# A hybrid S5 and sparse-attention decoder step: filler steps, row copies, key loads and attention side steps put in other places

## The chip, the cores and the metric

One NeuronCore of a Trainium2 chip runs the whole program. The metric is device time of one execution, in microseconds (us); lower is better. The engines are TensorE (PE for matmuls, PEld for its weight loads), VectorE (DVE), ScalarE (ACT), GpSimd (POOL) and SyncE (SP), which here issues nearly all DMAs.

## The reference

One step of a two-layer decoder on 256 new prompt tokens and 8 sample tokens (one for each of 8 sequences with 256 tokens of past), model width 1024, everything in fp32:

- Layer 0: RMS norm, an S5 mixer (64 groups of 16 channels, 64 complex states each, a scan over the 256 tokens), gelu, a gated linear unit (glu, 1024 to 2048), then a squared-ReLU MLP (1024 to 4096 to 1024).
- From its result come shared keys and values in three branches (compressed, selected, window), and queries and gates for layer 1.
- Layer 1: attention of 16 query heads on 4 key/value heads, three softmax branches weighted by sigmoid gates, an output projection and a second MLP.
- Outputs: the tokens, the new cache rows, the shifted window caches of the 8 sequences, and the S5 states.

The attention part, cut to its core:

```python
p_c = masked_softmax(q @ kc)          # 8 compressed blocks of 32 tokens
p_s = masked_softmax(q @ ks)          # selected blocks: with 256 tokens, all of them
p_w = masked_softmax(q @ kw)          # window of 512: all causal tokens
o = g[0] * (p_c @ vc) + g[1] * (p_s @ vs) + g[2] * (p_w @ vw)
win_kv_sample = concat([cache_win_kv, new_row])[:, -256:]    # 255 old rows are copied
```

## The kernel before, in words

**Dense work.** Every dense layer works on all 264 tokens at once, in tiles of 128 output features. `wload` (L594) issues a 512 KB weight load on SP into one of 4 `raw` buffers; `wsplit` (L601) splits it into a high part (ACT, L610) and a rest (DVE, L611); `mm3` (L616) makes three matmuls for each of 8 input blocks (L617 to L619). So a weight tile is 24 matmuls of 264 columns. MLP 0 and MLP 1 have 32 up tiles and 8 down tiles of 4 weight tiles each.

**The S5 stage** (`s5_stage`, L158) is written in a fixed order (`manual_schedule`). Beside it `sample_compress` runs as a generator, `filler(n)` being n steps of it. Its first three steps are loads; then come two streams (keys, values) of nine steps: eight with four matmuls each of cached page rows on the compression weights (L813), in four pairs, and one with biases and gelu. A pair of the first stream, when done, also issues the next weight load, and the second pair the sixteen page rows of a block (L789). `F` says how many steps stand where: `n` behind the first half's chunk matmuls (`chunk_in(0)`), `o` behind the second half's, `q` and `r` later. Behind `n` come `transpose_in(1)` and `chunk_in(1)`; behind `o` the output tables `powers_out` on DVE (L384 to L387), `kernels`, the scan tables, the scan (`up`, `carry`, `down`) and `from_states` (L483), which gives the stage's outputs. The first output table takes the buffer that `transpose_in(1)` reads from.

**Outside that stage** the compiler's planner orders each engine's instructions: it simulates the program with costs of its own and issues what is ready, earlier traced first, so a load whose buffer is free can move far ahead. `issue_after(i)` (here `after(engine)`, the engine's last traced instruction) keeps instructions behind another of the same engine.

**MLP 0** calls `side(m)` after each up tile: one step of `sample_keys` (two of `comp_tail`, then for each of 8 sequences 512 KB of cached keys, L862 and L864) for the first ten tiles, and for every odd m from 17 a copy of one sequence's old window rows from DRAM to DRAM (510 KB), behind SP's last load. It calls `on2(m)` after each down tile; for m = 1 that asks for the four compression weights of 512 KB (`compress_weights`, L1042).

**Before the attention stage** come the key/value tiles, the queries of group 0, the `gates` (L1106: one dense tile of 48 features, a sigmoid at L1118) and `Q1` of the four query tiles of group 1 (`q_dense`, L1135), with steps of the prompt's compression between them (`prompt_compress`, which has a gelu at L1074).

**The attention stage** (`prompt_attn`, L1164) goes through 12 units: for each of 2 groups and 2 head pairs a unit 0 (the first 128 tokens of both heads; scores at L1209 and L1213) and units for the second 128 tokens of each head (L1217, L1220). In round i it makes the scores of unit i, the softmax of unit i-1 (maximum at L1234 on DVE, exponentials at L1236 on ACT, scaling at L1245 on DVE), and transposes (L1254) and values (L1268, L1275) of unit i-2, then calls `side`. There are two score banks of PSUM, which a unit's exponentials set free. `cmp_branch` (L1178 to L1201) is the compressed branch of a group; group 1's must come before unit 6's values. `side` now drives two generators with the counts `SIDE` and `SIDB`: the first goes through the remaining query tiles, the two `q_post` (normalisation, rotary, transposes: two steps each) and `cmp_branch(1)`; the second through `sample_qk` (the sample's query and key norm; DVE lines L1304 to L1339) and the 12 steps of `sample_attn`: value loads and scores (L1381), softmax, transposes, values (L1424, L1428), for each of two halves of the sequences.

**After it** `out_proj` (L1450) makes 8 tiles; the first `SPLIT` = 3 have their group 0 half made early, between the last units. All need the sample's columns of `oh` and `ol`, which are split last in `sample_attn`.

Of the kernel before, what the change touches and what calls it, by code (L numbers as in the profile page):

```python
# [81 lines left out]
F32 = mybir.dt.float32  # L82
F32R = mybir.dt.float32r
I32 = mybir.dt.int32
AF = mybir.ActivationFunctionType
# [66 lines left out]
        pass  # L152


F = dict(n=4, o=5, q=4, r=5)


def s5_stage(K, filler):  # L158
# [356 lines left out]
    chunk_in(0)  # L515
    filler(F["n"])
    powers_in(1)
# [12 lines left out]
    bbar_block(1)  # L530
    filler(F["q"])
    kernels(1)
# [504 lines left out]
def compress_weights(K):  # L1037

    w1v = K.A["cmp_w1"]
    K.w1p = [e8(K, [128, 2, 4, 256], f"w1p{i}") for i in range(2)]  # L1040
    for lc in range(4):
        K.nc.sync.dma_start(K.w1p[lc // 2][:, lc % 2], w1v[0][:, 4 * lc:4 * lc + 4])  # L1042
# [63 lines left out]
def gates(K, xh, xl):  # L1106

    nc = K.nc
    S, V, G = nc.scalar, nc.vector, nc.gpsimd
    at, ak = K.at, K.ak  # L1110
    raw = K.wr.tile([128, 8, 48], F32, tag="raw", name="wg")
    nc.sync.dma_start(raw, K.A["w_gate"])
    pt = K.ps("mm")
    for k, h, l in wsplit(K, raw, parts=[(slice(0, 48), raw)]):
        mm3(nc, pt[0:48, 0:NT], h[:, 0:48], l[:, 0:48], xh[:, k], xl[:, k], k == 0, k == 7)
    g = ak.tile([48, NT], F32, name="gT")
    V.tensor_tensor(g, pt[0:48, 0:NT], K.rstd[0:48], ALU.mult)
    S.activation(g, g, AF.Sigmoid)  # L1118
    K.gp = at.tile([128, 2, 16, 3], F32, name="gp")
    pg = K.ps("tr")  # L1120
    for qt in range(2):
        nc.tensor.transpose(pg[:, 48 * qt:48 * qt + 48], g[:, 8 + 128 * qt:136 + 128 * qt], K.ident[0:48, 0:48])
    S.activation(K.gp.rearrange("p q h b -> p (q h b)"), pg[:, 0:96], AF.Copy)
    K.gs = at.tile([128, 2, 3], F32, name="gs")
    pg = K.ps("tr")
    for bh in range(2):
        lt = ak.tile([48, 4, 32], F32, tag="pct", name="glt", bufs=1)
        V.tensor_tensor(lt, g[:, 4 * bh:4 * bh + 4].unsqueeze(2).to_broadcast([48, 4, 32]),
                        K.cst("maskH")[0:48].unsqueeze(1).to_broadcast([48, 4, 32]), ALU.mult)
        nc.tensor.matmul(pg[:, 4 * bh:4 * bh + 3], lt.rearrange("p b h -> p (b h)"), K.cst("sel3")[0:48],  # L1130
                         start=True, stop=True)
    S.activation(K.gs, pg[:, 0:8].rearrange("p (b x) -> p b x", b=2)[:, :, 0:3], AF.Copy)
# [336 lines left out]
        part(m, (1,) if m < split else (0, 1))  # L1469


def build(ctx, tc, A, O):
    nc = tc.nc
    K = Ctx()
    K.nc, K.tc, K.A, K.O = nc, tc, A, O
    _, off = shape_constants()
# [32 lines left out]
    with ExitStack() as es:  # L1509
# [5 lines left out]
        steps = sample_compress(K)  # L1515
# [24 lines left out]
    with ExitStack() as es:  # L1540
        K.hid = es.enter_context(tc.tile_pool(name="hid", bufs=1))
        kh, kl = pair("kh", "kl", F32R)
        n2 = Norm(K)

        def on2(m):
            split_x(K, x[:, m], kh[:, m], kl[:, m], K.vec[:, 32 + m:33 + m])
            n2.add(x[:, m])
            if m == 1:
                compress_weights(K)
        K.ld = es.enter_context(tc.tile_pool(name="ld", bufs=2))  # L1550
        keys = sample_keys(K)

        def side(m):
            next(keys, None)
            if m == 10:
                with after(nc.gpsimd), after(nc.vector):
                    attn_tables(K)
            if m >= 16 and m % 2:
                b = (m - 16) // 2
                with tc.issue_after([i for i in nc.cur_bb.bb.instructions if i.engine == nc.sync.engine][-1]):  # L1560
                    nc.sync.dma_start(O["win_old"][b], A["cache_win_kv"][b, 1:256])
        mlp(K, 0, xh, xl, n1, x, on2, side)
    phase.close()
    psum(ctx, "pa", PSB)
# [1 line left out]
    with ExitStack() as es:  # L1566
# [3 lines left out]
        with ExitStack() as ek:  # L1570
# [46 lines left out]
            queue1 = []  # L1617
            q1 = q_dense(K, K.qh, K.ql, 1, queue1)
# [7 lines left out]
        oh, ol = ft(F32R, "oh"), ft(F32R, "ol")  # L1626
        with ExitStack() as ek:
            K.aa = ek.enter_context(tc.tile_pool(name="aa", bufs=1))

            def side_a(cmp_branch):  # L1630
                yield from q1
                for q in queue1:
                    yield from q
                cmp_branch(1)
                yield

            def side_b():
                sample_qk(K)
                yield
                yield from sample_attn(K, oh, ol)  # L1640
            steps = []

            def side(i, cmp_branch):
                if not steps:
                    steps.extend([side_a(cmp_branch), side_b()])
                for _ in range(SIDE[i]):
                    next(steps[0], None)
                for _ in range(SIDB[i]):
                    next(steps[1], None)
            prompt_attn(K, oh, ol, side)  # L1650
            for s in steps:
                for _ in s:
                    pass
        yh, yl = ft(F32R, "yh"), ft(F32R, "yl")
        n3 = Norm(K)
# [13 lines left out]
PSC = dict(fl=2, tr=3)  # L1669
PSA = dict(mm=3)  # L1670
PSB = dict(sc=2,po=1)
SIDE = (3,1,1,1,0,0,1,1,1,1,0,0,0,0)
SIDB = (1,2,2,2,2,2,2,2,0,0,0,0,0,0)
Q1 = 2
KVQ = 0
PLAN = ('cccc', 'qqq', 'qqq', 'qq', '', 'c', 'c', 'c', 'c', 'c', '', 'c', 'c', 'c', 'c', 'c')
SPLIT = 3
# [92 lines left out]
```

## Time and profile before

| what | us |
| --- | --- |
| runs | 745.57 median of 3, 744.51 to 746.26 |
| profiled execution | 747.1, its span 745.3 |
| PE busy (6160 matmul records) | 708.7 of the span, 95% |
| DVE, ACT, POOL busy | 526.0, 404.5, 55.7 |
| mean granted clock of PE | 0.956 |
| chain that ended last, by engine | PE 81%, DVE 10%, DMA 4% |

Times in the rows count from the span's start. The granted clock is the share of PE's full 2.4 GHz, so 0.50 is 1.2 GHz. Matmuls are pipelined, and a matmul's duration is longer than its distance to the next: the count of matmuls in a stretch says more of the pace than busy time. Roughly, the S5 stage ends at 106 us, glu at 153, MLP 0 at 350, keys, values and queries at 423, the attention stage at 538 and the rest with the end.

### The profile page before, as it was taken

What the parts mean: (1) busy time and instruction counts of PE and PEld (TensorE: products, weight loads), DVE (VectorE), ACT (ScalarE), POOL (GpSimd) and SP (SyncE); (2) the same over time, 40 slices, a digit from 0 to 9 for tenths busy, and PEclk for the clock granted to TensorE, in tenths of its full rate; (3) what the DMA queues carried; (4) which work ended last, traced back from release to release, by engine and by line L of the source; (5) the groups of instructions that cost most, each with busy time, mean ns of one, the idle gap of its engine ahead of it and who ended that gap; (6) DMA issues with size and microseconds to landing.
All of it is one profiled execution on the core that took longest, in us unless ns stands there. A gap on an engine that the chain in (4) does not pass through costs nothing.

```text
span 745.3 us, 16132 instructions
## 1 busy us (share of the span) xinstructions
PE 708.7 (95%) x6160; PEld 645.8 (87%) x6160; DVE 526.0 (71%) x1154; ACT 404.5 (54%) x918; POOL 55.7 (7%) x103
## 2 busy tenths in 40 slices
PE   3799879999999999999989989999999999999997
PEld 1788769999999999999978955455799999999997
DVE  8969988887677665656777698755488777755553
ACT  5339166656566554545664767444366666644442
POOL 0000001101200000001023141100030000000000
PEclk9699999999999999999999969577999999999999
DMA  7763117657997555555546551000165555565661
GB/s 252 224 183 129 58 60 227 193 166 229 382 320 266 185 185 184 178 191 171 178 158 211 162 183 58 0 1 1 57 195 173 176 191 171 185 192 191 198 188 40
DMA packets 53327, 124.68 MB, mean 167 GB/s; under 512 B 6522, under 2 KB 26874, under 8 KB 52994
## 3 DMA queue, kind: packets, MB, share of 16 engines
q1 hardware_dynamic: 52530, 122.08, 50.1%
q10 hardware_dynamic: 720, 1.58, 0.6%
q8 instruction: 48, 0.79, 0.5%
q14 instruction: 29, 0.24, 0.1%
HBM read 120.63 MB, written 7.18 MB: 171 GB/s over the span
## 4 chain that ended last, share of the span: by engine, by line
PE 81%; DVE 10%; DMA 4%; SPq 2%; issue 1%; ACT 1%; DVEq 0%; ACTq 0%
PE ps_mm L618 22%; PE ps_mm L617 22%; PE ps_mm L619 22%; PE ps_sc L1217 3%; PE ps_tr L1254 2%; PE ps_po L1275 2%; DMA w<-cmp_w_in 1%; DMA raw<-w_up_in 1%; DVE big L466 1%; DVE St L467 1%; PE ps_fl L813 1%; PE ps_mm L1428 1%; SPq L789 1%; PE ps_sc L1220 1%; DVE St L447 1%
## 5 line engine op out<-in xcount | busy, mean ns | idle before, releaser
L611 DVE TENSOR_TENSOR wl<-raw,wh 128x512 fp32r<-128x512 f32 x344 | 241.3, 706 | 147.5 <-ACT wh L610 141.5
L610 ACT ACTIVATE wh<-raw 128x512 fp32r<-128x512 f32 x344 | 215.1, 630 | 200.2 <-PE ps_mm L618 149.4
L617 PE MATMUL ps_mm<-hh,wh 128*128 128x264 f32 x512 | 145.3, 284 | 0.0
L618 PE MATMUL ps_mm<-hl,wh 128*128 128x264 f32 x512 | 145.0, 283 | 0.0
L619 PE MATMUL ps_mm<-hh,wl 128*128 128x264 f32 x512 | 145.0, 283 | 0.0
L618 PEld LDWEIGHTS ps_mm<-hl,wh 128*128 128x128 f32 x512 | 96.5, 188 | 0.0
L617 PEld LDWEIGHTS ps_mm<-hh,wh 128*128 128x128 f32 x512 | 96.4, 188 | 0.0
L619 PEld LDWEIGHTS ps_mm<-hh,wl 128*128 128x128 f32 x512 | 96.0, 187 | 0.0
L617 PE MATMUL ps_mm<-xhxl,wh 128*128 128x264 f32 x256 | 72.7, 285 | 1.2 <-ACT wh L610 1.2
L618 PE MATMUL ps_mm<-xhxl,wh 128*128 128x264 f32 x256 | 73.0, 285 | 0.0
L618 PE MATMUL ps_mm<-yl,wh 128*128 128x264 f32 x256 | 72.9, 285 | 0.0
L619 PE MATMUL ps_mm<-xhxl,wl 128*128 128x264 f32 x256 | 72.4, 284 | 0.4 <-DVE wl L611 0.4
L617 PE MATMUL ps_mm<-yh,wh 128*128 128x264 f32 x256 | 72.6, 284 | 0.0
L619 PE MATMUL ps_mm<-yh,wl 128*128 128x264 f32 x256 | 72.6, 284 | 0.0
L617 PEld LDWEIGHTS ps_mm<-xhxl,wh 128*128 128x128 f32 x256 | 48.2, 188 | 1.7 <-ACT wh L610 1.7
L619 PEld LDWEIGHTS ps_mm<-xhxl,wl 128*128 128x128 f32 x256 | 48.0, 188 | 0.9 <-DVE wl L611 0.9
L617 PEld LDWEIGHTS ps_mm<-yh,wh 128*128 128x128 f32 x256 | 48.2, 188 | 0.0
L619 PEld LDWEIGHTS ps_mm<-yh,wl 128*128 128x128 f32 x256 | 48.2, 188 | 0.0
L618 PEld LDWEIGHTS ps_mm<-xhxl,wh 128*128 128x128 f32 x256 | 48.1, 188 | 0.0
L618 PEld LDWEIGHTS ps_mm<-yl,wh 128*128 128x128 f32 x256 | 48.1, 188 | 0.0
L648 POOL TENSOR_TENSOR nacc<-nacc,sq 128x264 f32<-128x264 f32 x21 | 17.7, 844 | 322.1 <-ACT sq L647 241.4
L1236 ACT ACTIVATE P<-ps_sc,nm 128x128 f32<-128x128 f32 (+1 forms) x64 | 26.3, 427 | 26.9 <-DVE nm L1234 20.2
(438 smaller groups left out, 1471.2 us busy)
## 6 DMA issues: line engine op xcount, KB each, us to landing
raw<-w_up_in SPq DMA_DIRECT2D x64, 512.0 KB, 3.9
raw<-w_down_in SPq DMA_DIRECT2D x64, 512.0 KB, 3.6
raw<-s_w_glu_in SPq DMA_DIRECT2D x16, 512.0 KB, 3.7
w<-cmp_w_in SPq DMA_DIRECT2D x12, 512.0 KB, 4.5
raw<-w_kv_in SPq DMA_DIRECT2D x12, 512.0 KB, 3.7
blk<-cache_cmp_in SPq DMA_DIRECT2D x64, 64.0 KB, 2.1
raw<-w_q_in SPq DMA_DIRECT2D x8, 512.0 KB, 4.0
win_old_out<-cache_win_kv_in SPq DMA_DIRECT2D x8, 510.0 KB, 5.8
```

Source lines behind the costliest of these rows:

```text
L447: TT(o, o, b_, ALU.add)
L466: TT(w, c, m, ALU.mult)
L610: nc.scalar.activation(h[:, :, cols], src[:, c:c + 4], AF.Copy)
L611: nc.vector.tensor_tensor(l[:, :, cols], src[:, c:c + 4], h[:, :, cols].bitcast(F32), ALU.subtract)
L617: nc.tensor.matmul(out, wh, xh, start=start, stop=False)
L618: nc.tensor.matmul(out, wh, xl, start=False, stop=False)
L619: nc.tensor.matmul(out, wl, xh, start=False, stop=stop)
L648: nc.gpsimd.tensor_tensor(self.acc, self.acc, sq, ALU.add)
L1217: nc.tensor.matmul(banks[g2], K.QT[hs[g2], 4 * gp + 2 * rp + u - 1, 128:256], K.KTp[hs[g2], gp], start=True, stop=False)
L1236: S.activation(P[:, i], sv[:, i], AF.Exp, bias=nm[:, i:i + 1], accum_out=den[:, i:i + 1])
L1254: nc.tensor.transpose(pt[:, 128 * j:128 * j + 128], Pf[:, 128 * j:128 * j + 128], K.ident)
L1275: nc.tensor.matmul(po[64 * g2:64 * g2 + 64, 128 * kt:256], K.Vp[:, kt, br, 64 * g:64 * g + 64], rhs, start=False, stop=(br == 1 and kt == 1))
```

## The change

- `F`: two filler steps go from `n` to `o`.
- `gates`: an exponential of one element of the sigmoid's result follows the sigmoid on ACT; nothing reads it.
- The copies of old window rows go from MLP 0's up tiles 17, 19, ... 31 to its down tiles: tile m asks for the copy of sequence m, behind SP's last traced instruction.
- `sample_keys` makes a step after up tiles 0, 1, 2, 3 and then after every even tile, so the ten steps end at m = 14.
- `Q1` is 3: one more query tile of group 1 stands ahead of the attention stage.
- `SIDE` is now a table of letters for each round: a digit is a step of that `q_post`, `q` the last query tile (its PE instructions kept behind PE's last traced ones, the scores of unit 1), `s` is `sample_qk`, `a` a step of `sample_attn`, `d` is `cmp_branch(1)`. Compared with before, `sample_qk` goes from round 0 to 2, `sample_attn` from rounds 1 to 7 to rounds 4 to 10, and `cmp_branch(1)` from round 6 to 4.

```diff
-F = dict(n=4, o=5, q=4, r=5)
+F = dict(n=2, o=7, q=4, r=5)
...
     S.activation(g, g, AF.Sigmoid)
+    S.activation(ak.tile([1, 1], F32, name="tle"), g[0:1, 0:1], AF.Exp)
...
+def one(f, *a):
+
+    f(*a)
+    yield
...
             if m == 1:
                 compress_weights(K)
+            with after(nc.sync):
+                nc.sync.dma_start(O["win_old"][m], A["cache_win_kv"][m, 1:256])
...
         def side(m):
-            next(keys, None)
+            if m < 4 or m % 2 == 0:
+                next(keys, None)
...
-            if m >= 16 and m % 2:
-                b = (m - 16) // 2
-                with tc.issue_after([i for i in nc.cur_bb.bb.instructions if i.engine == nc.sync.engine][-1]):
-                    nc.sync.dma_start(O["win_old"][b], A["cache_win_kv"][b, 1:256])
...
-            def side_a(cmp_branch):
-                yield from q1
-                for q in queue1:
-                    yield from q
-                cmp_branch(1)
-                yield
-
-            def side_b():
-                sample_qk(K)
-                yield
-                yield from sample_attn(K, oh, ol)
-            steps = []
+            steps = {"s": one(sample_qk, K), "a": sample_attn(K, oh, ol)}
...
-                if not steps:
-                    steps.extend([side_a(cmp_branch), side_b()])
-                for _ in range(SIDE[i]):
-                    next(steps[0], None)
-                for _ in range(SIDB[i]):
-                    next(steps[1], None)
+                steps.setdefault("d", one(cmp_branch, 1))
+                for c in SIDE.get(i, ""):
+                    if c == "q":
+                        with after(nc.tensor):
+                            next(q1, None)
+                    else:
+                        next(steps[c] if c in steps else queue1[int(c)], None)
...
-SIDE = (3,1,1,1,0,0,1,1,1,1,0,0,0,0)
-SIDB = (1,2,2,2,2,2,2,2,0,0,0,0,0,0)
-Q1 = 2
+SIDE = {0: "0", 1: "q0", 2: "1s", 3: "1", 4: "ad", 5: "aa", 6: "aa", 7: "aa", 8: "aa", 9: "aa", 10: "a"}
+Q1 = 3
```

## Rows read from the trace of the kernel before

**Rows 1.** The page's second part: granted clock in 40 equal slices, tenths.

```profile
PEclk9699999999999999999999969577999999999999
```

**Rows 2.** Windows of the attention stage: length, then each engine's busy us, clock, DMA.

```profile
434.20:447.80 13.60, 13.60 (x31) 6.41 (x29) 13.13 (x50) 7.02 (x29) 7.58 (x14) 0.50 0.40 137
447.80:468.30 20.50, 19.31 (x123) 11.42 (x122) 17.20 (x53) 13.78 (x58) 3.57 (x13) 1.00 0.16 53
468.30:492.20 23.90, 23.32 (x80) 12.30 (x82) 13.05 (x39) 7.09 (x30) 1.36 (x1) 0.50 0.00 1
505.90:516.10 10.20, 10.20 (x47) 5.00 (x48) 4.99 (x17) 2.04 (x8) 0.00 (x0) 0.50 0.00 0
```

**Rows 3.** The chain of waits, S5 stage: start, length, what.

```profile
35.70 7.55 PE ps_fl L813 x32
43.25 0.45 PE ps_tr L350 x4
```

**Rows 4.** Timeline of PE, end of S5: start, length, what; idle before.

```profile
94.28 0.54 PE L483 MATMUL ps_mm<-St,Fb 128*32 128x72 f32 x21 [2.32 <-DVE St L467]
...
104.47 0.33 PE L483 MATMUL ps_fl<-St,Fb 128*32 128x72 f32 x8 [1.01 <-DVE St L467]
```

**Rows 5.** Timeline of ACT and DVE, S5's second half.

```profile
36.83 0.70 ACT L330 ACTIVATE E<-e 128x512 f32<-128x512 f32 x1
...
45.13 2.29 DVE L384 TENSOR_TENSOR Fc<-Cl,pr 128x2048 f32<-128x2048 f32 x1 [6.26 <-ACT ET L352]
```

**Rows 6.** Windows of MLP 0's up tiles.

```profile
195.00:210.00 15.00, 13.34 (x104) 12.49 (x103) 8.78 (x18) 8.38 (x20) 0.00 (x0) 1.00 0.99 385
230.00:245.00 15.00, 15.00 (x126) 15.00 (x125) 10.70 (x21) 9.61 (x22) 0.00 (x0) 1.00 0.79 269
```

**Rows 7.** Timeline of SP's DMA issues and of ACT, MLP 0.

```profile
191.07 3.95 SPq L1042 DMA_DIRECT2D w1p<-cmp_w_in  x4
195.11 0.99 SPq L597 DMA_DIRECT2D raw<-w_up_in  x2
197.01 0.63 SPq L1561 DMA_DIRECT2D win_old_out<-cache_win_kv_in  x1
...
204.72 0.63 ACT L610 ACTIVATE wh<-raw 128x512 fp32r<-128x512 f32 x1 [2.19 <-DMA raw<-w_up_in]
```

**Rows 8.** Timeline of ACT: table loads around the gates and the first softmax.

```profile
412.06 1.28 ACT L1118 ACT_TABLE_LOAD   x1
...
414.51 1.28 ACT L1074 ACT_TABLE_LOAD   x1
...
430.98 1.28 ACT L1236 ACT_TABLE_LOAD   x1
432.28 0.37 ACT L1236 ACTIVATE P<-ps_sc,nm 128x128 f32<-128x128 f32 x1
```

**Rows 9.** Timeline of PE in the attention stage: units 1 and 7, and transposes.

```profile
433.84 0.89 PE L1217 MATMUL ps_sc<-KTp,QT 64*128 64x512 f32 x1 [1.60 <-ACT P L1236]
...
445.14 1.91 PE L1254 MATMUL ps_tr<-ident,P 128*128 128x128 f32 x8
...
468.88 1.22 PE L1217 MATMUL ps_sc<-KTp,QT 64*128 64x512 f32 x1 [1.71 <-ACT P L1236]
```

**Rows 10.** Groups of DVE instructions by line, 430 to 450 us.

```profile
L1304 DVE TENSOR_SCALAR rs<-sv 128x96 int32<-128x96 int32 x1 | 1.2, 1211 | 0.0
...
L1333 DVE TENSOR_SCALAR ssq<-ssq,gvec 128x16 f32<-128x16 f32 (+1 forms) x3 | 0.6, 231 | 0.0
```

**Rows 11.** Timeline of PE and DVE: the sample's last steps and the output projection.

```profile
509.62 2.07 PE L1424 MATMUL ps_mm<-vnew,ptx 8*128 8x256 f32 x4
511.62 3.64 PE L1428 MATMUL ps_mm<-vr,pts 128*32 128x256 f32 x32
...
520.28 0.22 DVE L627 TENSOR_TENSOR ol<-os,oh 128x64 fp32r<-128x64 f32 x1
...
538.77 0.39 PE L617 MATMUL ps_mm<-oh,wh 128*128 128x264 f32 x1 [0.28 <-DVE x L1463]
```

**Rows 12.** Groups of PE instructions by line, 516 to 538 us.

```profile
L617 PE MATMUL ps_mm<-oh,wh 128*128 128x264 f32 x20 | 5.3, 297 | 0.0
```

More of the change, by code (lines that the diff above doesn't have):

```diff
@@ L1628, in build @@
             K.aa = ek.enter_context(tc.tile_pool(name="aa", bufs=1))
-            def side_a(cmp_branch):
-                yield from q1
-                for q in queue1:
-                    yield from q
-                cmp_branch(1)
-                yield
-            def side_b():
-                sample_qk(K)
-                yield
-                yield from sample_attn(K, oh, ol)
-            steps = []
-            def side(i, cmp_branch):
-                if not steps:
-                    steps.extend([side_a(cmp_branch), side_b()])
-                for _ in range(SIDE[i]):
-                    next(steps[0], None)
-                for _ in range(SIDB[i]):
-                    next(steps[1], None)
+            steps = {"s": one(sample_qk, K), "a": sample_attn(K, oh, ol)}
+            def side(i, cmp_branch):
+                steps.setdefault("d", one(cmp_branch, 1))
[5 more added lines that the diff above has]
+                        next(steps[c] if c in steps else queue1[int(c)], None)
             prompt_attn(K, oh, ol, side)
-            for s in steps:
-                for _ in s:
+            for _ in q1:
+                pass
+            for g in queue1 + [steps[c] for c in "dsa"]:
+                for _ in g:
                     pass
```

## The prediction, made before the result was known

> **What bounds the kernel now.** I read the page first. TensorE is busy for 708.7 of 745.3 us (the table of the profile above), so a saving must take away time in which PE waits or in which it runs slowly; the line of granted clock shows where the second lies: in the second slice, and in the 24th and the 26th to 28th, the attention stage [rows 1]. The windows cut at the changes of clock come next. Three stretches of 13.6, 23.9 and 10.2 us run at 0.50, the 1.2 GHz level, with PE busy almost throughout; those between them run at 2.4 GHz [rows 2]. So 47.7 us are worth 23.9 us if the clock stayed up and nothing else took over. DVE is the engine that would: 13.13 us of the first stretch's 13.6, but only 13.05 of the second's 23.9 and 4.99 of the third's 10.2 [rows 2]. Third, the first 106 us, where the order is written by hand: there DVE's long chain (output powers, scan tables, scan) ends last, and PE's last steps wait for it [rows 3 to 5]. Fourth, MLP 0, the only dense stage in which PE misses matmuls [rows 6].
>
> **The S5 tables.** Four filler steps (32 matmul records) run in 7.55 us on PE between the first half's chunk matmuls and the second half's transposes, 1.89 us a step [rows 3]. The change leaves two there and puts two, 3.78 us, behind the second half's chunk matmuls. The transposes, now at 43.1, could start at 39.5: their input, ACT's copy of E, ends at 36.83 + 0.70 = 37.5 [rows 5]. DVE's first output table had waited 6.26 us for them, until 45.13 [rows 5]; it starts near 41.4 and the DVE chain behind it moves up by 3.8. What is late next is PE: its own steps keep their sum, so its convolutions end where they did and only its waits for the scan can go. They are 2.32 us before the first state outputs and 1.01 us before the last [rows 4]. I take 3.3 us; the ends are 2.3 (the first wait alone) and 3.8 (all of DVE's move). The loads that the moved steps issue on SP (two weight tiles and sixteen page rows) go out up to 4 us later; they are for the second stream of page rows, which PE reaches four filler steps (7.6 us) and the first kernels later. That covers them, and without the cover the price is that same 4 us.
>
> **Row copies and key steps.** PE makes 104 matmuls in 195 to 210 us, where a quiet 15 us has 126 [rows 6]: 22 x 0.119 = 2.6 us lost. SP's order says why: four compression weights (2 MB) at 191.07, then two weight tiles at 195.11, which ACT gets at 204.72 after a wait of 2.19 us; the first row copy, at 197.01, stands behind those tiles [rows 7]. So taking the copies away from here doesn't free the tiles that stall. The new copies stand behind the last load of each down tile, one in 11.4 us (four weight tiles of 24 matmuls at 0.119); in 230 to 245 us they come twice as often and PE loses nothing [rows 6], so I cost them at nothing; were a weight tile held up behind one, the 2.6 us of now are the nearest price. One doesn't move as it seems: that of m = 1 is tied to SP's instruction before it, the last compression weight, which the planner already issues by 195 [rows 7], so it stays in the crowd. The key loads now come by every second tile; the planner issues them when a buffer is free, so their order on SP may hardly change. I take 0.6 us, nearest to the row order; ends +2.6 (the stall goes) and -2.6 (it doubles).
>
> **The attention stage.** No work is added but one exponential of one element. The third tile of the second query group goes ahead of the stage; the fourth (24 matmuls, 2.9 us) is held on PE behind unit 1's scores. Behind it on PE wait unit 2's scores; those first need unit 1's banks, so the tile lies in a wait that is there anyhow, and its query rows are first read by unit 9. If PE isn't waiting there, it costs nothing net either, as the same 2.9 us leave the time before unit 0. Now PE idles 1.60 us before unit 1's scores, waiting for ACT's exponentials, and the clock is at half in the stretch that follows [rows 2, 9]. A dense tile there should bring it back soon. DVE then binds: 13.13 us less the steps of the sample's query norm that move on by two units (1.2 + 0.6 us [rows 10]) is 11.3, so 13.6 can't go under 11.3: 2.3 us. In the second stretch the clock fell after a wait of 1.71 us for ACT before unit 7's scores [rows 9]; nothing is put there, and the sample's steps that come one by one are the same matmuls, later. I count that stretch and the third at nothing. Ends: all three at 2.4 GHz down to DVE's floor, 2.3 + 10.8 + 5.2 = 18.3 us gained; or the 20.5 us stretch falls to half, which costs the 19.3 us that PE is busy in it [rows 2]. I take 2.3, nearest to the stretch that the tile is put into.
>
> **The exponentials' table.** It is loaded at 430.98, 1.28 us, and the first exponential begins at 432.28, while PE stands idle [rows 8]. A tiny exponential behind the gates' sigmoid would move that load, but here the compression's gelu comes after the sigmoid (loads at 412.06 and 414.51 [rows 8]) and would throw the table out again. Then the load at 430.98 stays and one of 1.28 us is added where ACT isn't last. I take 0; ends +1.3 and -1.3. The Trainium skill (ScalarE: Activation LUTs, "Table sets: the hidden batching unit") says the same against this edit: each such function anchors a set of its own and calls are to be grouped by set. Its section "What ACT_TABLE_LOAD costs" puts a switch at 2.66 us, drain included; the row shows 1.30 from the load's start to the next function's, so by the page the ends would be twice as far.
>
> **Sum.** 3.3 + 0.6 + 2.3 + 0 = 6.2 us. The profiled execution took 747.1 (span 745.3 and 1.8 around it), so it would be 740.9; it is 1.5 over the median of the runs, 745.57, from which the same step gives 739.4.
>
> **The rivals.** (a) *The clock stays up further on.* If the calmer order also takes away the wait before unit 7, half of the 16.0 us in the second and third stretches comes on top: 739.4 - 8.0 = 731.4. For it: DVE has room there. Against it: nothing is put at that wait. (b) *Only S5 comes through.* The clock falls as now, or again between units 2 and 4, where the sample's score matmuls no longer stand: 745.57 - 3.9 = 741.7. For it: in the second stretch PE is busy for 23.3 of 23.9 us with scores and transposes and the clock stays down [rows 2]. The Trainium skill (TensorE: Matmul & The Clock Gate, "Part 4: PE-mode transpose") says that transposes don't count as PE-busy in the same way; by it this rival would be the likeliest at the same 741.7, but the rise at 447.8 came behind a stretch with eight transposes, at 445.14 [rows 9], so I don't raise it further. (c) *Slower: the sample's attention ends last.* Its steps begin at unit 4, not 1. Its outputs are split at 520.28, and the dense output projection starts at 538.77, 18.5 us later [rows 11]; within that, 20 x 3 projection matmuls, which need the sample's columns, fill PE between the last units [rows 12]. If the sample ends more than 18.5 us later against the units than now, that cover is gone. A unit takes 5.8 us (unit 1's scores at 433.84, unit 7's at 468.88 [rows 9]), so three use up 17.5 of the 18.5. From a fourth on it decides: 23.4 us, 4.9 too late, and 60 x 0.119 = 7.1 us of projection left over, 12.0 together, less the 5.6 us of sample matmuls that then no longer stand between the last units [rows 11]: +6.4. With S5's 3.3 that is 748.7. Against it: three units alone still fit. (d) *It doesn't do what it says:* the table is thrown out and the crowd on SP stays; that is the forecast less 0.6, 740.0. If the gelu comes before the sigmoid instead, 738.1.
>
> **How the numbers follow.** Forecast with (d), 737 to 741: 0.46. (a), 729 to 737: 0.18. (b), 741 to 744: 0.13. Small losses that eat the gain, within 0.2% of now (1.5 us, about what a measurement of this kernel can tell from no change): 0.08. (c), above 747.1: 0.15. So faster 0.77, same 0.08, slower 0.15. The range 731 to 747 leaves about half of (c) and a third of (a) outside, and lies inside the far ends of the clock; the likeliest case's own range is 736 to 742.
>
> **What would show it.** S5: the second transposes at about 39.5, the first output table at 41.4, the last state outputs about 3 us ahead of 104.47. Clock: the first half-clock stretch of the attention stage shorter than 13.6 us, with the tile of 24 in or ahead of it. Table: a load before the first softmax exponential, or none. MLP 0: still about 20 matmuls missing behind the compression weights. I am wrong if S5's shift comes out under 2 us, if the attention stage (115.1 us from 423.4 to 538.5) moves by more than 6 us either way, or if the sample's outputs are split after the last unit's values.

## The result and the profile after

The changed kernel takes 722.33 us (median of 4 runs, 718.70 to 723.78) against 745.04 for the kernel before, measured beside it: a ratio of 0.9716, 95% interval 0.967 to 0.976, so 18 to 25 us less. 739.4 was forecast, 731 to 747 as the range; the gain was more than three times as large as the forecast one, and the prediction was wrong. Executions of one kernel spread here with the clock that they were granted (the kernel before took 735.75 to 747.42 us in five sets of runs, at mean clocks of 0.969 to 0.949, the sets' medians lying between 742.80 and 745.38), so small terms are read from traces below and not from totals.

The profiled execution took 718.7 us, its span 716.9: 28.4 less than the profiled one of before. Two places hold this. Unit 0's scores begin at 415.16 instead of 423.36, 8.2 us earlier. (The change asks for one more query tile ahead of them, but the planner had put most of it there before: 186 of the 216 matmuls of queries and gates stood ahead of unit 0's scores, 192 do now, six more or 0.7 us.) The dense output projection begins at 505.91 instead of 538.77 [rows 11], 32.9 us earlier; of the 24.7 us between, 4.3 are given back, because 24 instead of 60 of its matmuls stand among the last units.

The granted clock in 40 slices of the changed kernel, to be held against [rows 1]:

```profile
PEclk9899999999999999999999989999999999999999
```

In place of four slices under 0.9 from the 24th on there is one. The windows of the attention stage, cut at the changes of clock (columns as in [rows 2]):

```profile
421.50:429.00 7.50, 7.34 (x19) 4.11 (x20) 7.45 (x37) 3.75 (x19) 1.31 (x2) 0.54 0.01 2
429.00:455.00 26.00, 26.00 (x148) 16.36 (x147) 22.07 (x70) 17.01 (x67) 9.63 (x27) 1.00 0.12 42
455.00:475.00 20.00, 19.52 (x145) 11.61 (x143) 17.79 (x58) 12.44 (x53) 1.08 (x2) 1.00 0.39 124
475.00:506.00 31.00, 31.00 (x254) 19.20 (x252) 17.52 (x51) 15.95 (x60) 0.00 (x0) 1.00 0.11 33
```

There were three stretches at 0.50, the 1.2 GHz level, of 13.6, 23.9 and 10.2 us [rows 2]; one is left, of 6.8 us within the first window. That is 40.9 us less at half speed, worth at most 20.5, which is near the attention stage's gain of 24.7 - 4.3 = 20.4 us (0.7 of it are the six query matmuls). What PE does at the two places (timeline: start, length, line, tiles, count; the wait before it in brackets):

```profile
419.48 1.93 PE L1179 MATMUL ps_po<-kcb,QT 128*128 128x16 f32 x16 [1.47 <-DVE vcm L1101]
421.66 1.97 PE L1218 MATMUL ps_sc<-KTp,QT 64*128 64x512 f32 x2 [0.25 <-ACT P L1237]
...
426.45 0.42 PE L617 MATMUL ps_mm<-qh,wh 128*128 128x264 f32 x1
...
455.84 1.12 PE L1218 MATMUL ps_sc<-KTp,QT 64*128 64x512 f32 x2 [0.48 <-ACT P L1237]
457.64 1.10 PE L1382 MATMUL ps_mm<-KTs,Qbd 128*32 128x265 f32 x16
459.70 1.12 PE L1218 MATMUL ps_sc<-KTp,QT 64*128 64x512 f32 x2
461.07 1.07 PE L1382 MATMUL ps_mm<-KTs,Qbd 128*32 128x257 f32 x16
```

The wait before unit 1 is 0.25 us instead of 1.60, and the one before unit 7 0.48 instead of 1.71 [rows 9]. A new wait of 1.47 us stands ahead of `cmp_branch(0)` (L1179), where it was 0.35. The held tile begins at 426.45, still at half clock, and the clock is back within it. Behind each half of unit 7's scores (455.84 and 459.70) stand 16 of the sample's score matmuls (L1382), which the texts below call dense. In the kernel before they stood ahead of unit 6, and the wait ahead of `cmp_branch(0)` was short:

```profile
430.02 1.93 PE L1178 MATMUL ps_po<-kcb,QT 128*128 128x16 f32 x16 [0.35 <-DVE vcm L1101]
...
454.85 1.99 PE L1381 MATMUL ps_mm<-KTs,Qbd 128*32 128x265 f32 x32
```

S5: the second transposes and the glu's first matmul on PE, then the first output table on DVE, beside [rows 3 to 5]:

```profile
36.88 1.95 PE L350 MATMUL ps_tr<-ident,E 128*128 128x128 f32 x16
...
102.38 0.39 PE L617 MATMUL ps_mm<-gh,wh 128*128 128x264 f32 x1
```

```profile
38.92 2.29 DVE L384 TENSOR_TENSOR Fc<-Cl,pr 128x2048 f32<-128x2048 f32 x1
```

The glu starts 4.1 us earlier than before (106.51), the table 6.2 us, more than the two moved steps are long; the early clock, below, is part of it. MLP 0 no longer misses matmuls where it missed 22 [rows 6]:

```profile
195.00:210.00 15.00, 15.00 (x125) 14.89 (x124) 10.51 (x21) 9.73 (x21) 0.00 (x0) 1.00 0.83 293
```

ACT's table loads, beside [rows 8]:

```profile
403.12 1.28 ACT L1118 ACT_TABLE_LOAD   x1
...
405.58 1.28 ACT L1074 ACT_TABLE_LOAD   x1
...
407.18 1.28 ACT L1119 ACT_TABLE_LOAD   x1
...
420.10 0.37 ACT L1237 ACTIVATE P<-ps_sc,nm 128x128 f32<-128x128 f32 x1 [1.76 <-DVE nm L1235]
```

The planner put the gelu between the sigmoid and the tiny exponential. So the exponentials' table is loaded last, in time, and no load stands before the first softmax.

### The profile page after: what moved, and what is told of

Same layout as the page of the kernel before. It is cut to its first block, busy times and chain, and to the rows that moved or that the text cites. A ratio compares the mean times of both kernels' runs of the same rounds, so it can differ in the third digit from the quotient of the medians.

```text
span 716.9 us, 16131 instructions
## 1 busy us (share of the span) xinstructions
PE 685.5 (96%) x6160; PEld 633.0 (88%) x6160; DVE 523.6 (73%) x1154; ACT 406.0 (57%) x919; POOL 63.9 (9%) x103
## 4 chain that ended last, share of the span: by engine, by line
PE 92%; DVE 4%; ACT 2%; issue 1%; DMA 0%; ACTq 0%; DVEq 0%
PE ps_mm L617 23%; PE ps_mm L618 23%; PE ps_mm L619 23%; PE ps_fl L813 4%; PE ps_sc L1218 3%; PE ps_po L1276 2%; PE ps_tr L1255 1%; PE ps_mm L410 1%; PE ps_sc L1214 1%; PE ps_sc L1221 1%; PE ps_mm L368 1%; PE ps_po L1269 1%; PE ps_mm L1382 1%; ACT P L1237 1%; PE ps_mm L1429 1%
## 5 line engine op out<-in xcount | busy, mean ns | idle before, releaser
L618 PE MATMUL ps_mm<-gl,wh 128*128 128x264 f32 x128 | 36.5, 285 | 0.0
```

Of the source, the lines that this page charges most:

```text
L618: nc.tensor.matmul(out, wh, xl, start=False, stop=False)
```

## The experiments

**First: is it the held tile, the spread of the sample's steps, or what lies ahead of the stage?** Four kernels.

`e1_att_only`: the kernel before with the attention part alone.

```diff
-SIDE = (3,1,1,1,0,0,1,1,1,1,0,0,0,0); SIDB = (1,2,2,2,2,2,2,2,0,...); Q1 = 2
+SIDE = {0: "0", 1: "q0", 2: "1s", 3: "1", 4: "ad", 5: "aa", ..., 10: "a"}; Q1 = 3
```

> The kernel before with only the attention part of the change: three query tiles ahead of the stage, the fourth held on PE behind unit 1's scores, the sample's and the side steps in their new rounds. Three theories of where the 22.7 us went. Theory T (the held tile): the 24 dense matmuls behind unit 1's scores end the first half-clock stretch early, and from there on PE has no wait long enough to lose the clock again. The traces give 20.2 us for the attention stage (28.4 between the two profiled executions less 8.2 by which unit 0's scores already began earlier), so about 725. Theory S (the spread): the sample's matmuls and cmp_branch, in later and earlier rounds, take away the wait before unit 7 and with it the second and third half-clock stretches; also about 725 here. Theory U (upstream): the attention stage keeps its clock because S5, MLP 0 and the table load changed what stands ahead of it; then the part by itself gives at most 3 us, 742 or more.

728.18 us against 744.53, ratio 0.981 (0.972 to 0.991). Its profile has one half-clock stretch in the stage, of 10.2 us. U falls as the only cause: 16.3 us by the medians (7 to 21 by the interval) come with this part by itself.

`e2_no_att`: the changed kernel with the old tables back (the diff above reversed).

> The changed kernel with the attention part undone: the old rounds and counts, two query tiles ahead of the stage, none held. S5, row copies, key steps and the tiny exponential stay. Theories T and S: only what lies ahead of the attention stage is left, 8.2 us by the start of unit 0's scores (4.1 in S5 from the start of the glu matmuls, 106.51 to 102.38, 2.6 in MLP 0, the rest after it), so about 737. Theory U: the gain stays, about 722 to 726.

733.24, ratio 0.987 (0.982 to 0.992), 10 runs from 727.33 at a mean clock of 0.979 to 736.66 at 0.963. So what lies ahead of the stage gives 11.3 us alone (6 to 14), more than the 8.2 of T and S. 11.3 + 16.3 is more than the whole 22.7, so the two may share a part; the intervals are too wide to show it. Its profile is one of the better runs. PE waits 1.70 us before unit 7, as before, and the clock stays up all the same:

```profile
450.32 1.99 PE L1382 MATMUL ps_mm<-KTs,Qbd 128*32 128x265 f32 x32
...
464.35 1.12 PE L1218 MATMUL ps_sc<-KTp,QT 64*128 64x512 f32 x2 [1.70 <-ACT P L1237]
```

```profile
425.50:446.00 20.50, 20.50 (x54) 11.65 (x55) 17.19 (x61) 9.88 (x43) 9.06 (x25) 0.50 0.41 132
446.00:518.00 72.00, 69.43 (x515) 43.67 (x516) 50.77 (x153) 38.59 (x155) 3.45 (x4) 1.00 0.09 30
```

That wait does not drop the clock every time, then; the same code falls in some executions and not in others.

`e3_no_tile`: the changed kernel, all four query tiles ahead of the stage.

```diff
-SIDE = {0: "0", 1: "q0", ...};  Q1 = 3
+SIDE = {0: "0", 1: "0", ...};   Q1 = 4
```

> The changed kernel with all four query tiles ahead of the attention stage, so that nothing dense is held behind unit 1's scores; the sample's and side steps keep their new rounds. Theory T: the first half-clock stretch is back at about 13.6 us instead of about 7, and one or both later ones with it: 3 to 20 us slower than the changed kernel, 726 to 742. Theory S: no later stretch at half the clock; the first may be longer by up to 7 us, worth 3.5: 722 to 726. Both overlap at 726, so the windows of granted clock decide: T wants half-clock pieces behind unit 4, S none.

725.93, ratio 0.979 (0.969 to 0.988). Windows of its stage:

```profile
424.50:442.00 17.50, 17.50 (x49) 10.33 (x49) 12.97 (x49) 9.46 (x41) 2.31 (x2) 0.51 0.05 18
442.00:509.00 67.00, 66.87 (x472) 39.73 (x471) 48.85 (x158) 37.99 (x152) 10.48 (x26) 1.00 0.16 49
```

The first stretch is long, no later one comes: the tile shortens the first, and the later ones go without it. T as a whole falls.

`e4_tile_only`: the changed kernel, tile held, all else nearly in the old rounds (the tables are shown against the kernel before).

```diff
+    if i == 1:
+        with after(nc.tensor):
+            next(q1, None)
...
-SIDE = (3,1,1,1,0,...)
+SIDE = (1,1,1,1,0,...)
-SIDB = (1,2,2,2,2,2,2,2,0,...)
+SIDB = (0,1,2,2,2,2,2,2,2,...)
```

> The changed kernel with the held query tile kept and the other attention steps back nearly in their old rounds (the sample's query norm in round 1, because it reads the held tile, its attention from round 2 with two steps in each, cmp_branch(1) last but one as before). Theory T: the clock comes back with the tile and stays: 720 to 726. Theory S: the first half-clock stretch is short, but a wait near unit 7 comes back and with it the later stretches of half clock, 24 and 10 us worth 17: about 733 to 739.

726.17, ratio 0.980 (0.970 to 0.989). The first stretch is within 424.0 to 431.5 as in the changed kernel, and a short one of 3.4 us comes from 465 on. Better than S said, and by its median just outside T's 726. But moved by even one round, the sample's score matmuls (L1382) stand at 451.4 to 455.75 here, among unit 6's scores, not ahead of them; so e4 is no clean opposite of e3.

**Second: the places themselves.** Idle matmuls fill one wait each; the tiny exponential is left out; the tile is moved.

`e5_pad_cmp`, the kernel before with:

```diff
+def pad(K, n):
+    with K.after(K.nc.tensor):
+        pt = K.ps("tr")
+        for _ in range(n):
+            K.nc.tensor.matmul(pt, K.identR, K.triR.unsqueeze(1).to_broadcast([128, 4, 128]), start=True, stop=True)
...
     # in cmp_branch, behind its score matmuls
+    gp or pad(K, 7)
```

> The kernel before with one addition: seven matmuls of 512 columns (about 1.6 us of PE at 2.4 GHz, at the 0.23 us that 512 columns take by the 0.119 us of a 264-column matmul), whose result nothing reads, held on PE directly behind cmp_branch(0)'s 16-column matmuls, where PE otherwise waits 1.6 us for unit 0's exponentials. Theory P (the place): in all six profiles so far the clock falls in or right behind cmp_branch(0), whether the wait behind it is 0.25 or 1.6 us, so what matters is that dense work stands there; the first stretch of 13.6 us shrinks to 7 or less, 3 to 5 us less, and the later stretches stay: 739 to 742. Theory W (the wait alone): the same, since the wait is filled. Theory N (none of it; the attention stage's gain comes from the order of the sample's steps): no change, 743 to 748. That the pad itself delays unit 1's scores, which wait for the exponentials until 1.6 us later anyway, would cost under 0.5.

747.13, ratio 1.006 (1.002 to 1.010): slower. The stretch shrank as P said, yet no time came of it:

```profile
428.50:432.00 3.50, 3.50 (x12) 2.92 (x12) 2.74 (x10) 3.49 (x16) 0.00 (x0) 0.51 0.99 324
432.00:466.00 34.00, 31.40 (x166) 17.25 (x165) 30.28 (x104) 22.39 (x93) 10.87 (x27) 1.00 0.25 79
466.00:487.00 21.00, 20.08 (x75) 10.02 (x75) 10.59 (x33) 4.73 (x18) 1.04 (x1) 0.51 0.00 1
```

In the 34 us behind it DVE is busy for 30.3 and PE misses 2.6: DVE takes over (before unit 2's scores PE now waits 1.18 us for it). The filler has a price of its own too, above the 0.5 us expected: unit 1's scores begin 5.34 us behind the start of `cmp_branch(0)`'s, 3.82 in the kernel before. And the late stretch comes as before. So the first stretch is not where the 20 us are.

`e6_pad_u7`, the kernel before with the same matmuls behind unit 6's scores:

```diff
-            sc[i] = scores(*units[i])
+            sc[i] = scores(*units[i]); i == 6 and pad(K, 7)
```

> The kernel before with the same seven matmuls held directly behind unit 6's scores instead, so that they lie ahead of the wait of 1.71 us before unit 7's scores and in it. Theory W: that wait is what drops the clock at 468.3, and filled, the second stretch of 23.9 us and the third of 10.2 go: up to 17 us, 728 to 734. Theory N: the clock falls there because of what PE does for long around it (scores and transposes), filled or not: 743 to 748, and up to 1.6 slower where the matmuls delay something.

736.16, ratio 0.991 (0.987 to 0.994): 7.7 us less by the medians (4 to 9 by the interval) for seven matmuls that compute nothing. In its profile, which is its best run (731.63), the first stretch is untouched and nothing falls behind it:

```profile
432.50:446.50 14.00, 14.00 (x32) 6.74 (x32) 13.24 (x51) 7.22 (x31) 7.68 (x14) 0.51 0.45 149
446.50:521.50 75.00, 73.82 (x536) 46.66 (x537) 51.73 (x160) 40.37 (x161) 4.56 (x14) 1.00 0.09 29
```

N falls; W's place is right, at less than half of its price over all runs (the other four have mean clocks of 0.967 to 0.971, so they still lose something, and no trace says where).

`e7_no_table`: the changed kernel without the line at L1119.

```diff
-    S.activation(ak.tile([1, 1], F32, name="tle"), g[0:1, 0:1], AF.Exp)
```

> The changed kernel without the tiny exponential behind the gates' sigmoid. In the changed kernel's trace the compression's gelu comes between the sigmoid and this exponential (table loads at 403.1, 405.6 and 407.2), so the exponentials' table is in place when the first softmax begins at 420.1; without it the load of 1.28 us lies ahead of that. Theory H (hidden): ACT idles 1.76 us there until the row maxima come, so the load hides: within 1 us of the changed kernel, 720 to 725. Theory L: the load comes only when the first exponential is ready and costs its 1.28 us, and the longer wait lets the clock stay down longer: 724 to 728.

724.55, ratio 0.974 (0.970 to 0.978), within both forecasts. The trace decides for L: the load stands behind ACT's wait for the row maxima, not in it, and PE's wait before unit 1 is 1.53 us, not 0.25:

```profile
424.15 1.28 ACT L1236 ACT_TABLE_LOAD   x1 [1.75 <-DVE nm L1234]
```

```profile
427.00 2.07 PE L1217 MATMUL ps_sc<-KTp,QT 64*128 64x512 f32 x2 [1.53 <-ACT P L1236]
```

The difference is the load's 1.28 us. The half-clock stretch behind it is 10.2 us here, not 6.8, with the tile in place.

`e8_tile_behind_cmp`: the changed kernel, tile inside `cmp_branch(0)`.

```diff
     # in cmp_branch, behind its score matmuls
+    if gp == 0:
+        with K.after(nc.tensor):
+            next(K.dense, None)     # the held query tile
...
-SIDE = {0: "0", 1: "q0", ...}
+SIDE = {0: "0", 1: "0", ...}
```

> The changed kernel with the held query tile moved from behind unit 1's scores to directly behind cmp_branch(0)'s 16-column matmuls. Theory P: the clock then doesn't fall there at all or for 3.4 us only, instead of 6.8: 1.5 to 2.5 us less than the changed kernel, 717 to 721; the tile takes 2.9 us there, of which 0.25 was a wait, so unit 1 is later by 2.6 and the units behind are as much earlier. Theory N: the place of the tile is without effect: 720 to 725. Against both: with unit 1 later, DVE, which binds behind it, starts its chain later: 724 to 727.

744.16 (730.84, and three from 743.81 to 745.22; too far apart for a ratio). All three expectations missed. In its profile the planner put the sample's score matmuls at 477.0, behind the second half of unit 7's scores, 9.1 us behind the start of the first (1.8 in the changed kernel), and a stretch of 30.7 us at half clock begins at 465.2. That made theory D: what matters is where these matmuls stand. It rests on one profile, and in that the clock falls ahead of unit 7's scores (467.89), so ahead of either place; it got its own test.

**Third: the terms, and theory D from both sides.**

`e9_s5_only`, the kernel before with:

```diff
-F = dict(n=4, o=5, q=4, r=5)
+F = dict(n=2, o=7, q=4, r=5)
```

> The kernel before with only the two filler steps moved. The prediction's term was 3.3 us; over the profiles so far the glu matmuls begin at 106.3 to 106.5 us without the move and at 102.4 to 103.5 with it. If the term is right: the glu at about 103, and 741.3 by the 744.5 that the kernel before takes. If the earlier attention stage lands luckier or not with its clock, the total is anywhere from 735 to 745 and only the glu's start tells.

741.05, ratio 0.997 (0.993 to 1.000): 1.8 us by the medians, 0 to 5 by the interval. The glu begins at 105.74, not at about 103. Over all profiles: mean 104.5 with the move (ten, 102.4 to 107.2), 107.1 without (six, 105.6 to 108.3), which is 2.5 us.

`e10_mlp0_only`: the copies and key steps of the change alone (its diff stands with the change).

> The kernel before with only the row copies and the key steps moved. The prediction took 0.6 us and the 22 missing matmuls in 195 to 210 us to stay. In the changed kernel they are gone. If that comes from this part: at most 7 of 126 missing there, 1.8 to 2.6 us, 742 to 743. If it came from the S5 shift instead, which moves MLP 0 against nothing else: 15 to 22 still missing, 744.5. The attention stage's clock can add up to 8 us to either side in the total; the count decides.

741.63, ratio 1.000 (0.996 to 1.004): nothing that totals show. The count, in its window of MLP 0:

```profile
195.00:210.00 15.00, 15.00 (x126) 15.00 (x125) 10.35 (x22) 9.52 (x21) 0.00 (x0) 1.00 0.91 352
```

None missing; but over all profiles the count varies: 22, 15, 8, 5, 3 and 8 missing without this part (mean 10), 0 to 10 with it (ten profiles, mean 4.5). That is 5.7 x 0.119 = 0.7 us, with ranges that overlap.

`e11_sample_late`: the changed kernel, the sample's first scores held behind unit 9's.

```diff
-... 4: "ad", 5: "aa", 6: "aa", 7: "aa", 8: "aa", 9: "aa", 10: "a"}
+... 4: "d", 9: "Aaa", 10: "aa", 11: "aa", 12: "aa", 13: "aaa"}   # A: as a, held like q
```

> The changed kernel with the sample's attention held back on PE from behind unit 7's scores to behind unit 9's, its twelve steps in rounds 9 to 13. Theory D (where the sample's dense score matmuls stand): in the profiles with no late half-clock stretch these 16 matmuls of 257 to 265 columns stand between unit 7's and unit 9's scores (or seven idle matmuls stand ahead of unit 7), and in those with one, of 20.5 to 30.7 us, they stand before unit 6 or two units later. So the late stretch comes back in most executions: 10 to 15 us slower, 732 to 738 and more if the sample then ends last. Theory T (the held query tile keeps the clock): no late stretch; only the tail, up to the 12 us by which the output projection can lose its cover, 722 to 734. The windows of granted clock between units 6 and 9 decide.

732.14, ratio 0.983 (0.975 to 0.992): 727.35 and 728.34 at clocks of 0.986 and 0.984, 735.93 at 0.972, and 742.91, the profiled one, at 0.961. In that the late stretch is back, with the tile in place and the wait before unit 7 as short as in the changed kernel:

```profile
460.98 1.12 PE L1218 MATMUL ps_sc<-KTp,QT 64*128 64x512 f32 x2 [0.49 <-ACT P L1237]
```

```profile
426.50:434.00 7.50, 7.25 (x19) 3.97 (x19) 7.44 (x37) 3.77 (x18) 1.26 (x1) 0.54 0.01 2
434.00:467.50 33.50, 33.01 (x183) 20.67 (x182) 29.03 (x87) 22.77 (x89) 10.79 (x28) 1.00 0.11 33
467.50:488.50 21.00, 21.00 (x57) 10.80 (x58) 10.62 (x32) 7.87 (x34) 0.00 (x0) 0.51 0.00 1
```

It comes in some executions, not in most as D said; the other two are 5 us slower at a clock as high as the changed kernel's, which fits the tail: in the profile the dense output projection begins at 525.70, 16.5 us behind the start of the last unit's values. It leans to D, no more, and D's premise has an exception: e2's profile has no late stretch either, with these matmuls ahead of unit 6.

`e12_before_sample_later`, the kernel before with one table changed:

```diff
-SIDB = (1,2,2,2,2,2,2,2,0,0,0,0,0,0)
+SIDB = (0,0,1,0,1,2,2,2,2,2,1,0,0,0)
```

> The kernel before with one table changed: the sample's query norm in round 2 and its attention in rounds 4 to 10, as in the changed kernel; both query tiles ahead of the stage, cmp_branch(1) in round 6, S5 and all else as before. Theory D: the sample's first score matmuls then stand directly behind unit 7's scores, the late half-clock stretches go, the first of 13.6 us stays: 730 to 736, 9 to 14 us less. Theory T: nothing dense is held, so the clock falls as before: 743 to 746.

731.71, ratio 0.985 (0.979 to 0.991), four runs within 731.12 to 733.18. As D said, and about half of the whole gain from moving the sample's steps alone. But W of e6, the wait alone, would give the same: unit 7's scores (their first half is the first row) no longer wait, and the sample's stand behind them:

```profile
469.61 1.12 PE L1217 MATMUL ps_sc<-KTp,QT 64*128 64x512 f32 x2
470.97 1.09 PE L1381 MATMUL ps_mm<-KTs,Qbd 128*32 128x265 f32 x16
```

```profile
433.50:447.50 14.00, 14.00 (x34) 7.23 (x33) 11.71 (x44) 6.94 (x28) 2.31 (x2) 0.51 0.01 4
447.50:484.50 37.00, 36.45 (x225) 22.04 (x224) 31.75 (x105) 23.61 (x94) 10.74 (x26) 1.00 0.18 58
484.50:488.50 4.00, 4.00 (x36) 1.55 (x34) 1.95 (x6) 1.51 (x8) 0.00 (x0) 0.57 0.00 0
```

The first stretch is as long as before; of the second and third 3.4 us are left.

**Fourth: the early clock, and the changed kernel again.**

`e13_s5_dense`, the changed kernel with:

```diff
+    pd = ps("mm")
+    for _ in range(3): nc.tensor.matmul(pd[:, 0:511], sameT, sqf[:, 0:511], start=True, stop=True)
```

> The changed kernel with three matmuls of 511 columns, whose result nothing reads, behind the five of the input norm in the S5 stage, where PE waits 4.57 us (17.45 to 22.02) for DVE's E; five records of such a matmul took 1.29 us each in two halves, so three fill 3.9 of it. In all fourteen profiles the clock falls right behind that wait and stays at half for 6.8 to 17.1 us of the next 18. Theory C (the wait drops the clock, and the half-clock stretch sets how much of the S5 move arrives): the stretch is gone or under 3.4, the glu begins at 101 to 102 instead of 102.4 to 105.7, and the time is 1 to 3 us under the changed kernel's of the same call. Theory N (the 73-column chunk matmuls behind it drop the clock in any case): the stretch stays, the time too.

723.08, ratio 0.972 (0.967 to 0.977). Over half of the wait is filled (2.04 us are left of it), the half-clock stretch stays, 13.6 us within this window, and DVE fills the window:

```profile
23.50:37.50 14.00, 12.74 (x167) 11.87 (x166) 13.41 (x24) 5.81 (x18) 0.00 (x0) 0.51 0.76 236
```

N holds: dense work ahead of light work does not carry the clock through it. Its 723.08 and the changed kernel's 724.12 have overlapping intervals, so no better version came of this.

`e14_changed_again`: the changed kernel itself.

> The changed kernel as it is, for comparison on the same chip, and for how often its clock falls late. By theory D the sample's score matmuls keep the clock from falling behind unit 6 in all or nearly all executions: every run under 728. If the good runs so far were luck with the clock alone, some should come at 730 or above, as 6 of 10 did with the old attention order behind the same S5 stage.

724.12, ratio 0.975 (0.970 to 0.980), six runs from 721.98 to 727.95 at clocks of 0.985 to 0.979; none at 730, against six of ten with the old attention order (e2). Its only half-clock stretch in the attention stage is the one at unit 1. So it was not luck of few runs.

## Why the prediction was wrong, step by step

**The failed step is the attention stage's second and third stretch:** "nothing is put there, and the sample's steps that come one by one are the same matmuls, later. I count that stretch and the third at nothing." Later was the point. The steps left the place ahead of unit 6, where the clock was high anyway, and came to stand behind unit 7's scores. The move also shortened the wait before unit 7, from 1.71 to 0.48 us, and to none in e12. Counted at 0, these two stretches are worth 11.1 us by e12 (7 to 16) and 7.7 by e6 (4 to 9). What was at hand for it: the letters of the new table, the score matmuls at 454.85 and the fall at 468.3 [rows 2]. I used them only in rival (b), as matmuls missing between units 2 and 4, and never asked where they would go.

**What stays open in it** is which of the two does it, the shorter wait or the dense matmuls. In the kernel before the clock falls at 468.3, in the wait ahead of unit 7's scores (468.88), and so in e9 and e10. Matmuls behind these scores come after that fall; what the move changes ahead of it is the wait, and e6's filler too lies ahead of it and cuts it to 0.73 us. Against the wait alone: e2 waits 1.70 us there without a fall, and in e11, with a wait of 0.49 and the sample's matmuls held back, the clock falls 6.9 us behind the start of unit 7's scores. Each of these is one profile.

**Rival (a)** named the condition (the calmer order takes away the wait before unit 7) and DVE's room, and its time, 731.4, is e12's. It had a chance of 0.18 and half of the price, and nothing else was added to it. **Rival (b)** held against the clock that it had stayed down with PE 98% busy; in that it was right for the kernel before. **Rival (c)** did not come: in the trace the sample's outputs are split at 499.8 and the dense projection starts at 505.9, 6.1 us of cover. **Rival (d)**, that the edits don't do what they say, failed in both halves.

**The first stretch:** 2.3 us by DVE's floor. It fell from 13.6 to 6.8 us with the tile and the table (10.2 with the tile alone, e1 and e7), worth at most 3.4. Over the profiles it is 6.8 to 10.2 us in the seven with the held tile and 13.7 to 20.5 in seven without it (e5 and e8 apart). What arrives of it no run shows by itself; e5 fits DVE's floor, with the filler's own price in it.

**The tile was put down as costing nothing net, and it cost something.** The sum let its 2.9 us leave the time before unit 0. In the kernel before it stood behind unit 0's scores, where it covered the wait for `vcm`: that wait ahead of `cmp_branch(0)` is 1.46 to 1.47 us in all seven profiles with the held tile, and 0.25 to 0.35 where no tile is held back.

**S5:** 3.3 us, ends 2.3 and 3.8; measured 2.5 by the glu's start, and 1.8 by e9's total (0 to 5). Right as far as that spread tells; the second transposes at 39.90 and the first output table at 41.93 in e14's profile are where they were expected. The 4.1 us of the profiled pair hold some luck with the early clock: in the stretch from 21 us on, the half-clock pieces add up to 6.8 us in the changed kernel's profile and 13.7 in its repeat.

**MLP 0:** 0.6 us, measured 0.7 by the counts, whose ranges overlap (3 to 22 missing without, 0 to 10 with it). The term is small, as said; more isn't shown. The account of it is half wrong: I expected about 20 matmuls to stay missing, none is in e10, and without this part they were never steady at 22. The copy of m = 1 stays where I said, right behind the compression weights, and does no harm there:

```profile
185.18 2.71 SPq L1042 DMA_DIRECT2D w1p<-cmp_w_in  x4
188.06 0.78 SPq L597 DMA_DIRECT2D raw<-w_up_in  x1
188.89 0.63 SPq L1558 DMA_DIRECT2D win_old_out<-cache_win_kv_in  x1
```

The seven other copies no longer stand there, and the key loads come in another order; which of the two frees the tiles was not tried apart.

**The table:** 0, ends 1.3 to both sides. The order was guessed wrong (the exponential came behind the gelu, not ahead of it), and the gain is the upper end, 1.28 us on PE's wait; with the shorter half-clock stretch it is 2.4 us (below). The Trainium skill (ScalarE: Activation LUTs, "What ACT_TABLE_LOAD costs") puts a switch at 2.66 us with the drain; here 1.28 is all that PE's wait lost.

**Sum:** by the medians 2.5 + 0.7 + 1.3 + 11.1 (e12) = 15.6, and e1 is 3.5 us below e12 (728.18 and 731.71; the intervals overlap): 19.1 of 22.7. The traces say more. From unit 0's scores to the end of the span it is 321.9 us in the kernel before (322.5 in e9), 309.0 in e12, 304.1 in e1, 304.2 in e7, and 301.7, 301.7 and 301.8 in the changed kernel, its repeat and e13. So in these profiles the sample's steps make 12.9 us, the rest of the attention part 4.9, and the tiny exponential 2.4. Ahead of it, unit 0's scores begin at 422.0 us on average in the five profiles with S5 and MLP 0 as before (420.5 to 423.4), and at 418.6 in eight with both changed (415.2 to 421.1; e3, with a tile more ahead, left out): 3.4 us. The 8.2 of the first pair set the latest beside the earliest.

What stays open: e2 gains 11.3 us without the attention part, though its terms make 4.5 (2.5, 0.7 and 1.3). Its profile has no late stretch and takes 308.9 us from unit 0's scores on, as e12's; why an earlier start with the same order makes these stretches rarer was not settled. That moving the sample's steps alone takes most of the late half clock away is shown (e12, four runs within 2.1 us), and that a filler ahead of unit 7 takes some of it (e6); that the absence of dense work there brings it back is only seen in one profile (e11).

## What to carry to other kernels

Where TensorE's clock falls for tens of us, list every dense group of matmuls that a change moves, with the time at which it stood and the one at which it will stand, and the waits that go with it, and hold them against the stretches at half clock: a move that adds no work can be worth more than all work that it saves. Filler paid here ahead of a stretch in which DVE had room (e6, DVE busy for 13 of 24 us), and not ahead of one that DVE filled (e5, 13 of 13.6). Look where a tile stands in the trace before moving it, as the planner may have moved it already, and look at several executions before one trace is made the base of a sum.

## What the runs showed of the hardware that was not expected

- The clock fell with hardly a wait: in e3 at 424.5, PE having waited 0.25 us, in the middle of `cmp_branch(0)`'s 16-column matmuls; and in the kernel before it stayed at half for 23.9 us with PE busy 98% of the time [rows 2]. In e2 a wait of 1.70 us passed without a fall. The Trainium skill (TensorE: Matmul & The Clock Gate, "Why this matters for your kernels") advises against idle gaps of PE between bursts of matmuls; e3's fall came without such a gap.
- The same program falls in one execution and not in the next: e2 took 727.33 us at 0.979 and 736.66 at 0.963, e8 730.84 at 0.979 and 745.22 at 0.955.
- A filled wait doesn't keep the clock by itself: e13's three matmuls of 511 columns ahead of the light S5 work left 13.6 us at half clock, e6's seven of 512 columns ahead of unit 7 left no late half clock in its profile.
- Seven matmuls that compute nothing, 1.89 us of PE, made a kernel 7.7 us faster by the medians, 4 to 9 by the interval (e6).
